# A two-layer hybrid decoder trunk on one core: the order of five engines written out, w1 in two halves, compressed keys in full columns

## The chip, the cores and the metric

The kernel runs on one core of one Trainium2 chip. The metric is the device time of one execution in microseconds (us), taken as the median over several runs. One execution was also recorded by the hardware profiler; every row below is from that record, with times counted from the start of its span.

The engines are called PE (TensorE: matmuls, with their weight loads shown as PEld), DVE (VectorE), ACT (ScalarE), POOL (GpSimd) and SP (SyncE, which here only starts DMAs).

## The reference

Two layers act on x (256 tokens x 1024). Each layer normalises x, projects it once (`z = h @ w_in`) and splits z among three groups of heads, whose gated outputs go through one output projection:

```python
h = rms_norm(x, norm_g); z = h @ w_in
o_a = fox_attention(fq, fk, fv, ff + fox_b) * silu(f_gate)        # 4 heads x 64, forget-gate bias
o_b = conformer_conv(glu_in, ...) * silu(c_gate)                  # GLU, 31-tap conv, LayerNorm, swish, pointwise
o_c = nsa_attention(nq, kc, vc, ks, vs, kw, vw, ...) * silu(n_gate)   # 8 query heads, 2 KV groups, 3 branches
x = x + concat(o_a, o_b, o_c) @ w_out                             # after both layers: a last rms_norm
```

The third group mixes, with sigmoid gates, three attentions: over 15 compressed blocks of keys and values, over selected blocks (with 256 tokens all four are selected) and over a window that here covers everything. The compression takes each 32-token block through a two-layer perceptron: `gelu(blk @ w1) @ w2`, with w1 of 2048 x 256 and w2 of 256 x 64, once for keys and once for values. Everything is float32.

## The kernel before, in words

**Precision by halves.** The large weights are split on the chip into a high part in the fp32r format (a cast on ACT, 128x1024) and a low part (a subtraction on DVE). A product is three matmuls: high x high, high x low, low x high. So every 512 KB block of weights passes one cast on ACT and one subtraction on DVE before PE uses it. `s(i)` is one such block of 128 columns of w_in: 24 matmuls of 256 columns into a PSUM bank that two consecutive `s` share. `mprod` does the same for blocks A and B, `project` for w_out.

**Buffers.** Raw weight blocks come in through SP into `RAW` = 6 buffers, in the order of `queue`; a block's buffer is given back when its low half is formed (`used(1)`), and then the next DMA may go. The blocks of w1 are used raw by PE in `compress(0)` (keys) and `compress(1)` (values), four blocks each, and given back as `compress` consumes them. `HILO` = 8 buffers hold the split halves. PSUM has two banks for `s` and the projections (tag z), three for scores (s), two for transposes (pt), one for attention outputs (o).

**A layer.** After A and B come the `s` blocks: convolution inputs (2 to 5), fox queries and keys (12 to 15), window and selection keys (6, 7), queries (8 to 11), compression inputs (0, 1), and the gates (16 to 23), with the work of the three head groups between them. The third group's attention runs in eight steps n: four heads for the first 128 tokens (t = 0), then four for the second. A step has scores on PE, a mask with maximum on DVE and an exponential on ACT (`exps`), a normalisation on DVE (`norms`), transposes on PE, a copy on ACT, and PV on PE, where `pv(n-1)` and `pv(n)` come together at every odd n. For t = 1 PE alternates these with `project`.

**What sets the order.** In the old kernel PE, SP and POOL follow the order in which the code is written. DVE and ACT do so in layer 0's opening only (the block up to `mprod(0, "B", NB)`); elsewhere a planner, which has its own estimates of durations, picks the order of these two. The forming of weight halves is asked for by `need`, which forms up to `AHEAD` blocks beyond the one wanted, and `behind` holds such an instruction behind marks set by `mark`. At the start PE runs `WARM` idle matmuls (`turn`): five, then eight transposes that spread the first norm gain, then three.

**Around the change.** PE's order there is `s(10)`, `compress(0)`, `fox_pv`, `compress(1)`, `s(11)`, `hidden`, then the first scores and the convolution. `compressed_kv` multiplies w2 with the perceptron's hidden values: for the keys, four matmuls that each fill 64 of PE's 128 columns (two groups, two halves of 256).

Of the kernel before, what the change touches and what calls it, by code (L numbers as in the profile page):

```python
# [9 lines left out]
F32 = mybir.dt.float32  # L10
# [9 lines left out]
AHEAD = 4  # L20
WARM = 5, 3
LAST = 416
LAG = 1
# [38 lines left out]
W2 = {"w2k": (0, 128), "w2v": (128, 128), "pw": (256, 512)}  # L62
W2_N = 768
# [63 lines left out]
def trunk(ctx, tc, a, out, dbg=None):  # L127
    nc = tc.nc
# [8 lines left out]
    ctx.enter_context(tc.manual_schedule(engines={E.SP, E.PE, E.Pool}))  # L137
# [33 lines left out]
    S_ORDER = (2, 3, 4, 5, 12, 13, 14, 15, 6, 7, 8, 9, 0, 1, 10, 11, "w1", 16, 17, 18, 19, 20, 21, 22, 23)  # L171
    queue = []
    parts = []
    for l in range(L):
# [5 lines left out]
        for i in S_ORDER:  # L180
            if i == "w1":
                for m in range(2):
                    for q in range(4):
                        queue.append((("w1", m, q, l), a["w1"][l, m, q], 1024))
# [11 lines left out]
    marks = [{}]  # L196

    def mark():

        at = {}  # L200
        for i in reversed(nc.cur_bb.bb.instructions):
            if i.engine in (E.DVE, E.Activation) and i.engine not in at and i.name not in formed:
                at[i.engine] = i
            if len(at) == 2:
                break
        marks.append(at)

    formed = set()

    def behind(engine, made):  # L210
        at = marks[-LAG].get(engine) if len(marks) >= LAG else None
        with tc.issue_after(at) if at is not None else nullcontext():
            made()
        formed.add(nc.cur_bb.bb.instructions[-1].name)

# [17 lines left out]
    def split_hi():  # L233

        key, n = parts.pop(0)
# [4 lines left out]
        behind(E.Activation, lambda: sc.copy(hi, w))  # L240
        split[key] = hi, lo

        def low():
            behind(E.DVE, lambda: ve.tensor_tensor(lo, w, hi.bitcast(F32), op=ALU.subtract))  # L244
            used(1)
        return low

    def split_next():
        if not parts or parts[0][0] not in raws:
            return False  # L250
        split_hi()()
        return True

    def need(key, ahead=AHEAD):

        while key not in split:
            assert split_next(), key
        n = sum(1 for k in split)
        while n < ahead + 1 and split_next():
            n += 1  # L260
        return split[key]
# [137 lines left out]
    for l in range(L):  # L399
# [17 lines left out]

        def mprod(t, which, n, steps="xt", p=None):
# [18 lines left out]
            if which == "A":  # L437
                sc.copy(vsw[:, t, :], p[:, :256])
                sc.activation(gl[:, t, :], p[:, 256:280], AF.Tanh, scale=0.5)
            else:  # L440
                sc.copy(fv[:, t, :], p[:, :256])
                ve.tensor_tensor(ff[:, t, :], p[:, 256:260], S("fb"), op=ALU.add)


        bank = {}

        def s(i, ahead=AHEAD):

            mark()
            hi, lo = need(("S", i, l), ahead)  # L450
# [11 lines left out]
        def s2(i):  # L462
            return bank.pop(i // 2).rearrange("p (i t) -> p i t", i=2)
# [27 lines left out]
        def gates(i):  # L491
            p = s2(16 + 2 * i)
            u = cp.tile([128, 2, 256], F32, name=nm(f"tg{i}"), tag="tg", bufs=1)
            sc.activation(u, p, AF.Tanh, scale=0.5)
            ve.scalar_tensor_tensor(sgt[0][:, 2 * i:2 * i + 2], u, 1.0, p, op0=ALU.add, op1=ALU.mult)
# [6 lines left out]
        def mix_split(c0, n, cols=slice(0, 256)):  # L502
            m = sgt[0][:, c0:c0 + n, cols]
            h = mixh[:, c0:c0 + n, cols]
            sc.copy(h, m)
            ve.tensor_tensor(mixl[:, c0:c0 + n, cols], m, h.bitcast(F32), op=ALU.subtract)
# [9 lines left out]

        def glu(i):

            p = s2(2 + 2 * i)
            th = cp.tile([128, 512], F32, name=nm(f"th{i}"), tag="tg", bufs=1)[:, 0:256]  # L520
            sc.activation(th, p[:, 1], AF.Tanh, scale=0.5)
            ve.scalar_tensor_tensor(ypad[:, i, 30:286], th, 1.0, p[:, 0], op0=ALU.add, op1=ALU.mult)
# [8 lines left out]
        def taps(i):  # L531
            if i == 0:
                sgt[0] = cp.tile([128, 2, 32, 32], F32, name=nm("cw"), tag="sg", bufs=1)
            cw = sgt[0][:, i]
            behind(E.DVE, lambda: ve.tensor_tensor(
                cw, C("sh").unsqueeze(1).broadcast_to([128, 32, 32]),
                S("cw")[:, i * 32:(i + 1) * 32].unsqueeze(2).broadcast_to([128, 32, 32]), op=ALU.mult))
            pconv[i] = pconv[i], cw.rearrange("p (g q) c -> p g q c", g=4)

        def conv():  # L540
            p = pscore(nm("pcn"))
            for i in range(2):
                yr, w = pconv[i]
                for q in range(8):
                    for g in range(4):
                        te.matmul(p[g * 32:(g + 1) * 32, i * 256:(i + 1) * 256], w[:, g, q], yr[:, g, 4 * q:4 * q + 256],  # L546
                                  start=q == 0, stop=q == 7)
            sgt[0] = cp.tile([128, 8, 256], F32, name=nm("sg"), tag="sg", bufs=1)
            for i in range(2):
                sc.activation(yc[:, i], p[:, i * 256:(i + 1) * 256], AF.Identity, bias=S("cb")[:, i:i + 1])  # L550
# [4 lines left out]
        def ln_stats():  # L555
            pt = ln["p"] = ppt(nm("lnp"))
            st = cp.tile([128, 2, 6], F32, name=nm("st"), tag="st", bufs=1)
            mv = ln["mv"] = cp.tile([128, 2, 2], F32, name=nm("mv"), tag="mv", bufs=1)
            rv = ln["rv"] = cp.tile([128, 2], F32, name=nm("rv"), tag="rv", bufs=1)
            for t in range(2):  # L560
                for c in range(2):
                    o = t * 256 + c * 128
                    te.transpose(pt[:, o:o + 128], yc[:, c, t * 128:(t + 1) * 128], C("id"))
            for t in range(2):
# [3 lines left out]
            gp.tensor_tensor(rv, rv, mhalf[:, :2], op=ALU.pow)  # L568
            yn = ln["yn"] = cp.tile([128, 2, 256], F32, name=nm("yn"), tag="rr", bufs=2)
# [4 lines left out]
        def ln_swish():  # L574
            yn = ln["yn"]
            pn = ppt(nm("lnq"))
# [4 lines left out]
            yl = cp.tile([128, 2, 256], F32, name=nm("yl"), tag="rr", bufs=2)  # L581
# [5 lines left out]
            ve.scalar_tensor_tensor(yt, yt, 1.0, yl, op0=ALU.add, op1=ALU.mult)  # L587

        def pointwise():
# [7 lines left out]
            return pcv.rearrange("p (i t) -> p i t", i=2)  # L597
# [15 lines left out]
        def forget():  # L613
            ffv = ff.rearrange("p t h -> p (t h)")
            lsr = cp.tile([128, 512], F32R, name=nm("lsr"), tag="ru", bufs=2)
            lsh, lsl = (lsr[:, c:c + 256].rearrange("p (t h i) -> p t h i", t=2, h=4) for c in (0, 256))
            fx["ls"] = lsh, lsl
            ve.scalar_tensor_tensor(fa, ffv, -1.0, ffv, op0=ALU.mult, op1=ALU.max)
            sc.activation(fe, fa, AF.Exp, scale=-1.0)
# [631 lines left out]
```

## Time and profile before

| | us |
|---|---|
| median of 3 runs | 316.83 (316.72 to 316.84) |
| the profiled execution | 316.37 |
| its span | 314.6 |
| PE busy | 303.7 |
| DVE busy | 234.9 |
| ACT busy | 186.9 |
| POOL busy | 22.6 |

The span runs from the first to the last recorded instruction; the time of the execution has some 1.8 us more around it. Matmuls overlap their neighbours, so the sum of single durations exceeds the busy time. Busy shares are averages over stages that have different limits, which is why the tables by stretch below matter more than the sums.

### The profile page before, as it was taken

How to read it: one execution, taken by the hardware profiler on the slowest of the kernel's cores; microseconds unless marked ns; L12 is line 12 of the kernel's file. 1: busy time of each engine (PE TensorE's matmuls, PEld its weight loads, DVE VectorE, ACT ScalarE, POOL GpSimd, SP SyncE). 2: the span in 40 equal slices, each digit the busy share in tenths (PEclk: the TensorE clock that was granted, in tenths of full speed). 3: DMA queues.
4: the chain of work that ended last, by engine and by line, in shares of the span. 5: the costliest groups of instructions: out<-in, count | busy, mean ns of one | idle time of the engine just before them, and what ended most of it. 6: DMA issues, size and time to landing. Idle time of an engine off the chain costs nothing.

```text
span 314.6 us, 6713 instructions
## 1 busy us (share of the span) xinstructions
PE 303.7 (97%) x2596; PEld 273.8 (87%) x2596; DVE 234.9 (75%) x626; ACT 186.9 (59%) x408; POOL 22.6 (7%) x49
## 2 busy tenths in 40 slices
PE   7999999999999999999999999999999999999991
PEld 5799999995789999888899999999578999988891
DVE  3957689981999998965574778998199989896532
ACT  4757668731595957861545766783259595786110
POOL 2000043000002000000000003400000200000000
PEclk9999999999999999999999999999999999999998
DMA  7797889707927445130461878880792744000101
GB/s 285 256 382 272 277 246 236 290 2 271 409 69 258 133 135 155 46 94 2 166 200 70 292 233 258 219 307 2 285 403 59 260 135 133 0 2 0 63 8 69
DMA packets 16545, 54.93 MB, mean 175 GB/s; under 512 B 2048, under 2 KB 2560, under 8 KB 16512
## 3 DMA queue, kind: packets, MB, share of 16 engines
q1 hardware_dynamic: 15264, 51.29, 46.9%
q0 software_dynamic: 960, 2.92, 4.1%
q8 instruction: 20, 0.33, 0.4%
q10 hardware_dynamic: 288, 0.28, 0.3%
q14 instruction: 13, 0.11, 0.1%
HBM read 52.85 MB, written 1.64 MB: 173 GB/s over the span
## 4 chain that ended last, share of the span: by engine, by line
PE 88%; issue 4%; DMA 4%; DVE 1%; ACT 1%; POOLq 0%; POOL 0%; DVEq 0%
PE ps L457 15%; PE ps L458 14%; PE ps L459 14%; PE pcn L546 4%; PE pA L430 4%; PE pt L915 4%; PE pB L430 4%; PE pw L982 4%; PE pw L979 4%; PE pw L978 4%; PE on L928 3%; DMA ww<-in_w 3%; PE sw L859 2%; PE sw L860 2%; DMA cf<-in_cf 1%
## 5 line engine op out<-in xcount | busy, mean ns | idle before, releaser
L457 PE MATMUL ps<-hTh,wS_1h 128*128 128x256 f32 x192 | 54.3, 283 | 0.0
L457 PE MATMUL ps<-hTh,wS_0h 128*128 128x256 f32 x192 | 54.3, 283 | 0.0
L459 PE MATMUL ps<-hTh,wS_1l 128*128 128x256 f32 x192 | 53.9, 281 | 0.0
L458 PE MATMUL ps<-hTl,wS_0h 128*128 128x256 f32 x192 | 53.9, 281 | 0.0
L459 PE MATMUL ps<-hTh,wS_0l 128*128 128x256 f32 x192 | 53.9, 281 | 0.0
L458 PE MATMUL ps<-hTl,wS_1h 128*128 128x256 f32 x192 | 53.9, 281 | 0.0
L887 ACT ACTIVATE P<-P,mx 128x128 f32<-128x128 f32 (+1 forms) x64 | 28.5, 447 | 15.1 <-DVE mx L482 15.0
L457 PEld LDWEIGHTS ps<-hTh,wS_1h 128*128 128x128 f32 x192 | 36.2, 188 | 0.6 <-issue 0.4
L457 PEld LDWEIGHTS ps<-hTh,wS_0h 128*128 128x128 f32 x192 | 36.2, 188 | 0.6 <-issue 0.4
L458 PEld LDWEIGHTS ps<-hTl,wS_1h 128*128 128x128 f32 x192 | 36.2, 188 | 0.2
L458 PEld LDWEIGHTS ps<-hTl,wS_0h 128*128 128x128 f32 x192 | 36.2, 188 | 0.2
L459 PEld LDWEIGHTS ps<-hTh,wS_1l 128*128 128x128 f32 x192 | 36.2, 188 | 0.0
L459 PEld LDWEIGHTS ps<-hTh,wS_0l 128*128 128x128 f32 x192 | 36.2, 188 | 0.0
L244 DVE TENSOR_TENSOR wS_0l<-wS,wS_0h 128x1024 fp32r<-128x1024 f32 x24 | 28.6, 1221 | 8.4 <-ACT wS_0h L240 8.4
L244 DVE TENSOR_TENSOR wS_1l<-wS,wS_1h 128x1024 fp32r<-128x1024 f32 x24 | 28.5, 1221 | 8.1 <-ACT wS_1h L240 8.1
L240 ACT CAST wS_1h<-wS 128x1024 fp32r<-128x1024 f32 x24 | 24.1, 1051 | 1.8 <-DMA wS<-in_wS 1.8
L240 ACT CAST wS_0h<-wS 128x1024 fp32r<-128x1024 f32 x24 | 24.1, 1049 | 0.5 <-DMA wS<-in_wS 0.4
L482 DVE CUSTOM_DVE_ANT_0 P<-sw,cf 128x128 f32<-128x128 f32 (+1 forms) x64 | 19.5, 355 | 2.4 <-PE sw L860 2.4
L917 ACT COPY PT<-pt 128x512 f32<-128x512 f32 x24 | 13.6, 586 | 9.6 <-PE pt L915 9.6
L985 DVE TENSOR_TENSOR x<-pw,x 128x512 f32<-128x512 f32 (+1 forms) x9 | 5.7, 631 | 16.8 <-PE pw L982 16.8
L485 DVE TENSOR_SCALAR P<-P,co 128x128 f32<-128x128 f32 (+1 forms) x64 | 16.4, 316 | 0.1
L546 PE MATMUL pcn<-yr,cw 128*32 128x256 f32 x256 | 14.2, 380 | 0.0
(239 smaller groups left out, 679.3 us busy)
## 6 DMA issues: line engine op xcount, KB each, us to landing
wS<-in_wS SPq DMA_DIRECT2D x48, 512.0 KB, 5.7
ww<-in_w SPq DMA_DIRECT2D x16, 512.0 KB, 5.3
wO<-in_wo SPq DMA_DIRECT2D x16, 512.0 KB, 4.0
yr<-ybuf POOLq DMA_DIRECT2D x16, 142.0 KB, 5.0
wA<-in_wA SPq DMA_DIRECT2D x4, 420.0 KB, 4.2
wB<-in_wB SPq DMA_DIRECT2D x4, 390.0 KB, 5.0
x<-in_x SPq DMA_DIRECT2D x2, 512.0 KB, 4.1
w<-in_w SPq DMA_DIRECT2D x2, 384.0 KB, 4.7
```

What stands on the lines that cost most here:

```text
L240: behind(E.Activation, lambda: sc.copy(hi, w))
L244: behind(E.DVE, lambda: ve.tensor_tensor(lo, w, hi.bitcast(F32), op=ALU.subtract))
L430: te.matmul(p[:, :n], a_[:, k, tok], b_, start=first, stop=s_ == "t" and k == 7)
L457: te.matmul(o, hi[:, k], hTh[:, k], start=k == 0, stop=False)
L458: te.matmul(o, hi[:, k], hTl[:, k], start=False, stop=False)
L459: te.matmul(o, lo[:, k], hTh[:, k], start=False, stop=k == 7)
L482: ve.tensor_tensor_reduce(o, x, m, -1.0, 3.0e38, ALU.add, ALU.min, mx)
L485: ve.tensor_scalar(x, x, r, None, op0=ALU.mult)
L546: te.matmul(p[g * 32:(g + 1) * 32, i * 256:(i + 1) * 256], w[:, g, q], yr[:, g, 4 * q:4 * q + 256], start=q == 0, stop=q == 7)
L887: sc.activation(P[:, g, b], P[:, g, b], AF.Exp, bias=mx[:, c:c + 1], scale=-1.0, accum_out=su[:, c:c + 1])
L915: te.transpose(pt[:, o + b * 128:o + (b + 1) * 128], Pg[:, b * 128:(b + 1) * 128], C("id"))
L917: sc.copy(PT, pt)
```

## The change

Five things change.

The first and largest: the order of DVE and ACT is written out for the whole kernel too, and every helper that did work on several engines is cut into pieces that can be placed one by one (`exps` into `mask` on DVE and `expo` on ACT, `norms` into `coeff` and `norms(n, g)`, `trans` into transposes and `ptcopy`, `gates` into `gate_tanh` and `gate_mul`, `query` into `query_rope` and `query(i, g)`, and so on). `need`, `mark` and `behind` go; each half of a weight block is formed where `form_hi` or `form_lo` stands.

```diff
-    ctx.enter_context(tc.manual_schedule(engines={E.SP, E.PE, E.Pool}))
+    ctx.enter_context(tc.manual_schedule(engines={E.SP, E.PE, E.Pool, E.DVE, E.Activation}))
-WARM = 5, 3
+WARM = 8, 1
-    S_ORDER = (2, 3, 4, 5, 12, 13, 14, 15, 6, 7, 8, 9, 0, 1, 10, 11, "w1", 16, 17, 18, 19, 20, 21, 22, 23)
+    S_ORDER = (2, 3, 4, 5, 12, 13, 14, 15, 6, 7, 0, 1, 8, 9, 10, "w1a", 11, "w1b", 16, 17, 18, 19, 20, 21, 22, 23)
...
+    def form_hi():
+        key, n = parts.pop(0)
...
+        sc.copy(hi, w)
+        lows.append((lo, w, hi))
+    def form_lo():
+        if lows:
+            lo, w, hi = lows.pop(0)
+            ve.tensor_tensor(lo, w, hi.bitcast(F32), op=ALU.subtract)
+            used(1)
```

The second: the eight blocks of w1 are queued in two halves with S11 between them, and PE's order follows. S0 and S1 come before S8 and S9. This is the new order around it:

```diff
+        s(8)
+        fox_copy(0, 0)
+        blocks(0)
+        fox_copy(0, 1)
+        form_lo()
+        blocks(1)
+        fox_trans(1, 0)
+        fox_trans(1, 1)
+        form_hi()
+        s(9)
+        fox_copy(1, 0)
+        fox_copy(1, 1)
+        form_lo()
+        s(10)
+        query_rope(0)
+        keys_hi()
+        fox_pv()
+        query(0, 0)
+        query(0, 1)
+        compress(0)
+        keys_lo(0)
+        keys_lo(1)
+        s(11)
+        part(0)
+        taps(0)
+        taps(1)
+        compress(1)
+        query_rope(1)
+        part(1)
+        hidden()
+        query(1, 0)
+        scores(0)
+        load_w2()
+        scores(1)
+        form_hi()
+        conv(0)
+        mask(0, 0)
+        expo(0, 0)
+        branch_gates()
+        mask(0, 1)
+        query(1, 1)
+        expo(0, 1)
+        form_lo()
```

Here `taps` (the convolution's weights, on DVE), `branch_gates` (DVE) and the load of w2 have later places than before. The written order of the steps up to the exponentials of step 3, and of the last two steps, is:

```diff
+        s(19)
+        norms(2, 1)
+        compressed_v()
+        form_lo()
+        ln_back()
+        pv(0)
+        swish_in()
+        mask(3, 0)
+        mask(3, 1)
+        pv(1)
+        trans(2, 0)
+        trans(2, 1)
+        scores(4, (0,))
+        s(20)
+        swish()
+        ptcopy(2)
+        expo(3, 0)
+        expo(3, 1)
+        form_hi()
+        coeff(3)
+        norms(3, 0)
...
+        cmp_norm(1)
+        trans(6, 0)
+        form_lo()
+        trans(6, 1)
+        proj0(1, (0, 1))
+        ptcopy(6, 0)
+        ptcopy(6, 1)
+        coeff(7)
+        norms(7, 0)
+        form_hi()
+        proj0(1, (2, 3))
+        norms(7, 1)
+        form_lo()
+        cmp_trans(1)
+        cmp_copy(1)
+        trans(7, 0)
+        residual(0, 0, 512, pj[0])
+        trans(7, 1)
+        proj0(1, (4, 5))
+        ptcopy(7, 0)
+        ptcopy(7, 1)
+        load_g(a["norm_g"][1] if l == 0 else a["final_g"], nm("gn"))
```

The third: the keys' w2 is stored twice side by side (w2k of 256 columns in place of 128), so that two matmuls with all 128 columns do the work of four with 64; two small copies on ACT pick each group's part.

```diff
-            for g in range(2):
-                for m in range(2):
-                    te.matmul(pk[g * 64:(g + 1) * 64, 0:16], w2k[:, m], gk[:, m, g * 16:(g + 1) * 16],
-                              start=m == 0, stop=m == 1)
+            for m in range(2):
+                te.matmul(pk[:, 0:32], w2k[:, m], gk[:, m], start=m == 0, stop=m == 1)
...
+            kcp = cp.tile([128, 16], F32, name=nm("kcp"), tag="kcp", bufs=1)
+            for g, (r, r2) in enumerate(halves):
+                sc.copy(kcp[r], pk[r, g * 16:(g + 1) * 16])
+            kc = rope(kcp, C("cc"), C("sc"), (16,), "kc")
```

The fourth: the idle matmuls at the start are eight and one in place of five and three. The fifth: `pv(0)` and `pv(1)`, and so on in pairs, stay side by side on PE but with DVE's and ACT's pieces written between them; the last projection's two halves of 256 columns (`proj2`) run all high products of eight k before the low ones.

## Rows read from the trace of the kernel before

**Rows 1.** The page: engines with busy us, share and instructions; PE in 40 slices.

```profile
PE 303.7 (97%) x2596; PEld 273.8 (87%) x2596; DVE 234.9 (75%) x626; ACT 186.9 (59%) x408; POOL 22.6 (7%) x49
...
PE   7999999999999999999999999999999999999991
```

**Rows 2.** Waits: who waited for what, us in total, times, longest us.

```profile
PE ph L791 <- DMA ww<-in_w: 1.3, 2, 0.6
PE g0p L288 <- DMA cf<-in_cf: 1.3, 1, 1.3
```

**Rows 3.** PE in order of time, the compression: start us, us, instruction, [idle before].

```profile
71.23 1.93 PE L791 MATMUL ph<-ww,xp 128*32 128x256 f32 x32
...
74.55 1.59 PE L791 MATMUL ph<-ww,xp 128*32 128x256 f32 x24
76.78 0.64 PE L791 MATMUL ph<-ww,xp 128*32 128x256 f32 x8 [0.65 <-DMA ww<-in_w]
...
80.29 0.97 PE L808 MATMUL hidT<-cf,part 128*128 128x32 f32 x8
```

**Rows 4.** Windows: stretch, length, busy by engine; two `s`, then the two compressions.

```profile
40.98:43.82 2.84, 2.84 (x26) 2.84 (x25) 2.84 (x4) 1.90 (x5) 1.18 (x3) 1.00 1.07 229
77.35:80.29 2.94, 2.94 (x28) 2.94 (x25) 1.16 (x1) 2.39 (x3) 0.00 (x0) 1.00 1.03 414
71.23:73.09 1.86, 1.86 (x33) 0.93 (x32) 0.69 (x2) 0.00 (x0) 0.00 (x0) 1.00 0.29 31
74.55:77.35 2.80, 2.15 (x34) 0.73 (x33) 0.00 (x0) 0.00 (x0) 0.00 (x0) 1.00 1.03 420
```

**Rows 5.** SP's DMA issues in order of time.

```profile
47.71 10.12 SPq L225 DMA_DIRECT2D ww<-in_w  x6
...
71.93 0.80 SPq L225 DMA_DIRECT2D ww<-in_w  x2
```

**Rows 6.** ACT and DVE in order of time, around and after the compression.

```profile
77.49 0.37 ACT L796 COPY part<-ph 128x256 f32<-128x256 f32 x1 [3.88 <-PE ph L791]
79.13 1.23 DVE L244 TENSOR_TENSOR wS_0l<-wS,wS_0h 128x1024 fp32r<-128x1024 f32 x1 [7.20 <-ACT wS_0h L240]
```

**Rows 7.** The chain that ended last, in order of time: start us, us, what.

```profile
93.77 0.35 PE pkv L830 x8
94.12 0.59 PE pkv L833 x4
155.78 0.87 PE hp L354 x8
```

**Rows 8.** Windows: the dense stretch; columns as in rows 4.

```profile
80.50:138.70 58.20, 58.20 (x546) 51.52 (x546) 54.97 (x192) 42.62 (x111) 1.64 (x1) 1.00 0.48 160
```

**Rows 9.** The head: a window, then instructions in order of time.

```profile
7.74:12.70 4.96, 4.56 (x29) 3.25 (x27) 4.39 (x9) 3.01 (x5) 0.55 (x1) 1.00 0.84 306
6.22 1.41 DVE L338 SCALAR_TENSOR_TENSOR h<-x,rs,g0p 128x512 f32<-128x512 f32 x2 [0.67 <-POOL rs L332]
6.32 1.62 PE L282 MATMUL turn<-idle 128*128 128x512 f32 x3
6.84 0.89 ACT L240 CAST wA_0h<-wA 128x840 fp32r<-128x840 f32 x1 [0.39 <-DMA wA<-in_wA]
8.40 1.07 ACT L356 CAST hTh<-hp 128x512 fp32r<-128x512 f32 x2 [0.67 <-PE hp L354]
9.02 0.69 DVE L360 TENSOR_TENSOR hTl<-hp,hTh 128x512 fp32r<-128x512 f32 x1 [0.47 <-ACT hTh L356]
```

**Rows 10.** DVE and PE in order of time: operations that the change moves.

```profile
18.71 0.23 DVE L611 TENSOR_SCALAR gate<-gate,cf 128x8 f32<-128x8 f32 x1
...
120.41 3.49 DVE L244 TENSOR_TENSOR wO_0l<-wO,wO_0h 128x1024 fp32r<-128x1024 f32 x3
140.41 1.17 PE L915 MATMUL pt<-cf,P 128*128 128x128 f32 x8
```

**Rows 11.** DMA issues of the page: KB each, median us from issue to landing.

```profile
gn<-in_norm_g SPq DMA_DIRECT2D x1, 512.0 KB, 7.4
```

More of the change, by code (lines that the diff above doesn't have):

```diff
@@ L61 @@
 SM_N = _o
[L62 to L63 removed]
+W2 = {"w2k": (0, 256), "w2v": (256, 128), "pw": (384, 512)}
+W2_N = 896
 CF = {}
@@ L195, in trunk @@
     raws, split, held = {}, {}, [0]
[L196 to L214, printed above, removed]
     def pump():
@@ L231, in used @@
         pump()
-    def split_hi():
+    lows = []
+    def form_hi():
+        if not parts:
+            return
         key, n = parts.pop(0)
@@ L1051, in trunk @@
[L1051 to L1068 removed]
+        bias_rows()
+        form_hi()
+        s(15)
+        bias_heads()
+        form_lo()
+        form_hi()
+        s(6)
+        fox_k()
+        form_lo()
@@ new lines, in trunk @@
+        mask(1, 0)
+        scores(2)
+        expo(1, 0)
+        mask(1, 1)
+        s(16)
+        form_lo()
+        expo(1, 1)
+        ptcopy(0)
+        coeff(1)
+        norms(1, 0)
+        norms(1, 1)
+        form_hi()
+        ln_trans()
+        form_lo()
+        compressed_kv()
+        s(17)
+        ln_stats()
+        form_hi()
+        mask(2, 0)
+        mask(2, 1)
+        expo(2, 0)
+        expo(2, 1)
+        form_lo()
+        trans(1, 0)
+        trans(1, 1)
+        scores(3)
@@ new lines, in trunk @@
+        expo(3, 0)
+        expo(3, 1)
+        form_hi()
+        coeff(3)
+        norms(3, 0)
+        cmp_scores(0)
+        gate_tanh(1)
+        norms(3, 1)
+        form_lo()
+        scores(4, (1,))
+        form_hi()
+        s(21)
+        cmp_soft(0)
+        gate_mul(1)
+        form_lo()
+        pointwise()
+        mask(4, 0)
+        gate_tanh(2)
+        gate_mul(2)
+        expo(4, 0)
+        trans(3, 0)
+        cmp_norm(0)
+        trans(3, 1)
+        mask(4, 1)
+        form_hi()
@@ new lines, in trunk @@
+        gate_tanh(3)
+        form_lo()
+        pv(3)
+        expo(5, 1)
+        pv_cmp(0)
+        gate_mul(3)
+        trans(4, 0)
+        coeff(5)
+        form_hi()
+        trans(4, 1)
+        norms(5, 0)
+        scores(6, (0,))
+        ptcopy(4, 0)
+        norms(5, 1)
+        proj0(0, (0, 1))
+        mixed(4, 4, on[0], 0.5, TA)
+        ptcopy(4, 1)
+        mix_hi(4, 4, TA)
+        mask(6, 0)
+        mix_lo(4, 4, TA)
+        form_hi()
+        scores(6, (1,))
+        proj0(0, (2, 3))
@@ new lines, in trunk @@
+        form_lo()
+        expo(6, 0)
+        mask(6, 1)
+        trans(5, 0)
+        expo(6, 1)
+        trans(5, 1)
+        form_lo()
+        scores(7, (0,))
+        ptcopy(5, 0)
+        proj0(0, (4, 5))
+        ptcopy(5, 1)
+        coeff(6)
+        norms(6, 0)
+        norms(6, 1)
+        form_hi()
+        scores(7, (1,))
+        cmp_soft(1)
+        proj0(0, (6, 7))
+        form_lo()
+        form_hi()
+        pv(4)
+        mask(7, 0)
+        expo(7, 0)
+        pv(5)
+        mask(7, 1)
```

724 lines of the change are left out of this document (395 added, 329 removed).

## The prediction

> **What bounds the kernel now.** I read the page's first two parts first: PE is busy 303.7 of 314.6 us, nine tenths or more in 38 of 40 slices, and DVE 234.9 us, unevenly spread [rows 1]. A kernel like this gets shorter only by what leaves PE's queue or by PE's own waits. So the second view is what PE and its weight loads waited for: two entries of over a microsecond, the w1 load and cf at the head [rows 2]. PE in order of time shows where: `compress(0)` and `compress(1)` are the same 32 matmuls, and the second breaks off after 24 of them until a DMA lands [rows 3]. Cut to those stretches, the table of windows gives the price: 1.86 us for the undisturbed run, 2.80 for the disturbed one, so 0.94 us a layer, 1.88 in both (the second layer's rows repeat the first's) [rows 4]. The remaining PE idleness is at the head (start to 12.7 us) and behind the last matmul (307.8 to the end), and the change leaves the tail's chain as it is. Everything else in PE's queue touches: a step of `s` follows the one before. So the gain to be had is near 3 us, and the question is whether five hand-written orders give some of it back.
>
> The sum is made against the profiled execution, 316.37 us (span 314.6 and 1.8 around it). The median of the runs is 316.83, 0.46 more, added at the end. With each term stand its ends, the least and the most that it may cost.
>
> **w1 in two halves.** Now six of the eight w1 blocks are issued from 47.7 us on, as raw buffers come free, and the last two only at 71.93, when `compress(0)` has consumed its first block [rows 5]. The last block is in PE at 76.78, 5.55 us after `compress(0)` began (71.23), and the queue moved 420 GB/s meanwhile, which is 1.25 us for a 512 KB block [rows 3, 4]. After the change S11's matmuls stand between the two compressions. The written order forms the low halves of S10 and S11 ahead of `s(10)`, so again two w1 blocks wait for `compress(0)` and no more. Their need moves: `compress(1)` begins 1.86 + 2.94 (an `s` behind narrow matmuls, 77.35 to 80.29 [rows 3]) = 4.80 us after `compress(0)` and needs its last quarter at 4.80 + 3/4 of 1.76 = 6.1 us. Against 5.55 the block is there with 0.57 us to spare. The term: -1.88 us. Its other end: if buffers are handed out in fixed turns, a third block waits, the last lands 1.25 later at 6.8, and 0.7 us of wait stays per layer (term -0.5).
>
> **What this order costs behind it.** `hidden` used to come a whole `s(11)` after `compress(1)`; now it comes at once and reads the copy `part`. That copy starts 77.49 and takes 0.37 [rows 6], so it ends 0.51 us after PE could have gone on at 77.35; `hidden` is eight records in 0.81 us, of which the first half reads the older half of `part` and covers 0.40. I take 0.25 us per layer with the first weight load exposed; ends 0 and 0.6. PE also changes once more between narrow and full column groups: an `s` behind narrow matmuls takes 2.94 against 2.84 behind another [rows 3, 4], so 0.1 per layer; ends 0 and 0.2. Together +0.7.
>
> **Compressed keys in full columns.** Four narrow matmuls (eight records, 0.35 us, 0.044 each) become two full ones (four records). The full ones beside them take 0.117 to 0.15 each [rows 7], so 0.45 to 0.59 against 0.35: 0.1 to 0.24 dearer; on the other side the change of column groups on the way in and out goes, about 0.1 each by the `s` pair above. I take 0; ends -0.25 and +0.25 per layer. The two additional copies of 64x16 on ACT cost less than `part`'s 0.37 each (128x256 [rows 6]). ACT is busy 42.6 of 58.2 us there [rows 8], and the compressed scores come two `s` later; uncovered they would cost up to 0.7 per layer.
>
> The Trainium skill, "TensorEngine Tiling (Array Packing)", section "When to Use Tiling", speaks against this edit: a result of at most 64 columns should be column-tiled for twice the throughput. By it the full form would cost as much again as the narrow one, +0.35 us per layer; the trace's neighbour says 0.1 to 0.24 before the saved switches.
>
> **Head.** The idle turns go from 5 + 3 to 8 + 1. Five turns end with PE waiting 1.27 us for cf; three more at 0.43 each just fill that. After the eight transposes three turns run 6.32 to 7.74 while the first half of h is scaled at 6.92 (6.22 plus half of 1.41): the transposes wait for the turns [rows 9]. With one turn PE is free at 6.9. The high copy of hT on ACT could then start when the cast before it ends, 6.84 + 0.89 = 7.73, not 8.40: up to 0.67. DVE is the tighter one: the low half, at 9.02, finds DVE idle for 0.47 only, since the mean square that ends 8.55, so it and the scale of the second token block behind it move by 9.02 - 8.60 = 0.42, and so do the next transposes (11.37) and everything after. Term -0.42; ends -0.67 and +1.5 (rival C).
>
> **Five written orders.** PE's list is otherwise the old one: s0 and s1 trade places with s8 and s9, `fox_pv` goes ahead of `compress(0)`, and PV already ran in pairs (pv(0) and pv(1) side by side). None of these changes a count, so I cost them at nothing; what hides them is that each operand is ready early. In the front of the layer the two `taps` go out of DVE's way, into its 7.20 us hole before 79.13 [rows 6], and the first fox transposes find their norms about 2 us early by the list.
>
> The dense stretch is 80.5 to 138.7, where DVE works 54.97 of 58.20 us [rows 8]. Now the written order must do there: the same, plus S16's low half (1.23, at 79.13 now [rows 6]) and the branch gates (0.81 for four [rows 10]), less O7's low half and the residual (1.15 and 0.60; three low halves in 3.49 give the first [rows 10]), so 55.3 us. It may start when s(11) ends (80.29 now), after the change a compression earlier; from there to the transposes of step 7, which now start at 140.41 [rows 10], PE has 60.1 + 1.9 + 0.2 = 62.2 us. 6.9 us may be lost to waits in order, against 3.2 now. Going down the written list with these durations I find about 6: 1.5 before the first scores, 1.7 for the swish that waits for `ln_back` behind s(19), 1.5 for the exponentials of step 3 behind the swish on ACT, the rest in pieces. What waits behind those on DVE are low halves and norms due only 1 to 3 us later. So `norms(7)` comes in 0.9 us ahead of its transposes: no PE wait, a small margin. Term 0; ends 0 and +2.5 per layer.
>
> **DMAs moved.** `load_w2` (448 KB for 384) goes from ahead of `compress(0)` to behind `compress(1)`, some 80 us in; at the norm gain's 7.4 us from issue to landing, which was queued in the same place [rows 11], it is there by 88 and needed at 93.8 [rows 7]. The norm gain moves to step 7, behind O7's buffers, about 141.5 + 7.4 = 149; its scaling feeds transposes at 155.8 [rows 7], so nothing; without that cover DVE's queue would stand up to 2 us with the residual behind it.
>
> **Sum.** -1.88 + 0.70 + 0 - 0.42 + 0 + 0 = -1.60; 316.37 - 1.60 = 314.77, and + 0.46 = 315.2 us. Its own range, from the small ends: 314.3 to 316.2.
>
> **Rivals.** A, the slower side: the written DVE order loses more in waits than the planner's, and step 7's transposes wait. Until 0.9 us of delay it is free; beyond that each us costs 2 (two layers). For it: 94% busy DVE, a list that can't take what is ready. Against: the earlier start. With 2.2 us more lost: 315.2 + 2 x 1.3 = 317.8; it makes the kernel slower from about 2.1 us. B: the w1 wait stays because a third block waits, -0.5 in place of -1.88: 316.6. For it: the last block's margin is only 0.57. Against: two slots came free before `compress(0)` in the old order too. C: with one turn PE idles before the first transposes, and the clock's rise comes later. The turns at 6.32 run 0.47 apart where 512 columns later need 0.23, the pace of 1.2 GHz against 2.4; PE's busy time from 7.74 to 12.70 is 4.56 us [rows 9], of which I let a third be paid twice: +1.5 and the 0.42 lost, 317.1. Against: eight turns fill the idle 1.27 us ahead of it. D, the good side: `hidden` and the switches cost nothing and the head gives 0.67, 315.2 - 0.95 = 314.2.
>
> **Chances.** Forecast 0.54, A 0.19, B 0.12, C 0.05, D 0.10. A difference of 0.2% (0.63 us) is what a measurement here can tell: faster is below 316.2, slower above 317.5. Faster: forecast less its edge, and D, 0.61. Within: B, C and that edge, 0.20. Slower: A, 0.19. Range 313.9 to 318.0: D's end to a little beyond A.
>
> **What would show it.** Right: `compress(1)` a run of 1.9 us with no DMA wait; the first transposes near 7.0 and s(2) 0.4 earlier; a gap under 0.4 ahead of `hidden`'s second half; no DVE wait before the transposes of step 7. Wrong: PE idle ahead of any `trans`, a wait for ww in either layer, or a PE wait on ACT in the first fox scores, which I cost at nothing.

## The result, and the profile after

The changed kernel took 315.05 us (median; 313.70 to 319.48) where the kernel before took 317.25 in the same call: ratio 0.992, 95% interval 0.9901 to 0.994. Measured again beside the first experiments it took 314.07 us (313.46 to 315.88) against 317.65, ratio 0.9891 (0.9863 to 0.9919). By the two ratios it is faster by 2.5 and 3.5 us; the intervals reach from 0.6 to 1.4%. The forecast was 315.2 us; its gain over the kernel before was 1.6. Three of its first twenty executions were longer (318.6 to 319.5 us, at a lower mean clock) and are left out of the ratio; the first record is of one of them, so the rows below are from the second record, of 315.88 us, span 314.1, where nothing else is said.

In the rows, `ph` are the compression's matmuls, `ww` its w1 blocks, `fs`, `fP` and `fpt` the fox scores, probabilities and transposes, and `hidT` the matmuls of `hidden`. The page has the same picture as before [rows 1]. PE is busy nearly everywhere, and its busy time is 0.5 us less:

```profile
PE 303.2 (97%) x2589; PEld 274.2 (87%) x2589; DVE 240.3 (77%) x626; ACT 186.9 (59%) x412; POOL 20.8 (7%) x49
...
PE   7999999999999999999999999999999999999991
```

What PE's queue lost and won is seen only in its stretches. These are the windows of the key compression, s(11) and the value compression in layer 0, then both compressions in layer 1 (start to end, length, busy by engine, clock, DMA share, GB/s); they answer to [rows 4]:

```profile
72.54:74.40 1.86, 1.86 (x38) 0.98 (x34) 1.76 (x4) 1.25 (x3) 0.00 (x0) 1.00 0.00 0
74.40:77.45 3.05, 3.05 (x31) 2.83 (x24) 2.74 (x3) 0.37 (x1) 0.00 (x0) 1.00 0.94 334
77.45:79.31 1.86, 1.86 (x35) 1.02 (x33) 1.52 (x4) 0.00 (x0) 0.00 (x0) 1.00 1.01 401
...
220.87:222.73 1.86, 1.86 (x38) 0.99 (x34) 1.76 (x4) 1.29 (x3) 0.00 (x0) 1.00 0.00 0
225.74:228.58 2.84, 2.21 (x35) 0.82 (x33) 2.47 (x5) 0.00 (x0) 0.00 (x0) 1.00 1.03 417
```

In layer 0 the value compression is a clean 1.86 us, 0.94 less than before, as forecast. In layer 1 of this execution it is 2.84 again. The instructions in order of time say why, and they show a second wait that the record of the kernel before does not have, in the first fox scores (start, length, instruction, [idle before, and who ended it]):

```profile
52.01 0.22 PE L691 MATMUL fs<-fk,fq 128*128 128x128 f32 x1
52.91 0.33 PE L692 MATMUL fs<-fklz,fq 128*128 128x128 f32 x1 [0.68 <-POOL fklz L669]
...
221.09 1.93 PE L803 MATMUL ph<-ww,xp 128*32 128x256 f32 x32
225.96 1.64 PE L803 MATMUL ph<-ww,xp 128*32 128x256 f32 x24
228.24 0.64 PE L803 MATMUL ph<-ww,xp 128*32 128x256 f32 x8 [0.63 <-DMA ww<-in_w]
```

The last w1 block was late in layer 1: PE had it 7.15 us after `compress(0)` began (221.09 to 228.24), where the prediction took 5.55 and a margin of 0.57. And POOL's zeroing of the fox keys' low parts (`fklz`) was late, by 0.68 us in layer 0 and 0.21 in layer 1.

The first record (319.48 us) has the same w1 wait in a worse form, two blocks late in layer 1 of the changed kernel; behind it the granted clock is 0.50 of the full 2.4 GHz, the lower level of 1.2, after PE had worked only 1.8 of the 3 us from 225 to 228 (the last row is a window, columns as above):

```profile
227.59 0.64 PE L803 MATMUL ph<-ww,xp 128*32 128x256 f32 x8 [1.17 <-DMA ww<-in_w]
228.85 0.83 PE L803 MATMUL ph<-ww,xp 128*32 128x256 f32 x8 [0.62 <-DMA ww<-in_w]
...
231.00:234.00 3.00, 3.00 (x19) 2.50 (x22) 1.82 (x12) 1.76 (x6) 0.00 (x0) 0.50 0.99 391
```

From the start of `compress(0)` to the first transposes of step 0 layer 1 took 21.2 us, where layer 0 of the same record has 15.9. It is one record; how often this comes is not shown.

For the late zeroing, POOL's queue and SP's:

```profile
50.11 2.19 POOL L506 DMA_DIRECT2D yr<-ybuf  x4 [9.77 <-DMA ybuf<-ypad]
52.34 1.09 POOL L669 MEMSET fklz<- 64x512 f32 x2
```

```profile
38.39 14.01 SPq L203 DMA_DIRECT2D ww<-in_w  x4
```

Before, the same store of the convolution's input came back after 4.42 us and the zeroing ran from 48.80:

```profile
46.58 2.18 POOL L527 DMA_DIRECT2D yr<-ybuf  x4 [4.42 <-DMA ybuf<-ypad]
48.80 1.09 POOL L673 MEMSET fklz<- 64x512 f32 x2
```

The first w1 block is issued at 38.4 where it was 47.7 [rows 5]. I took these early w1 loads for what slows the store, but two runs speak against it. With the w1 edit undone (below) the first w1 block goes at 47.55 again, and the store still takes 7.97 us, in layer 1 9.69. And with the head edit alone, in the planner's order (below), it takes 7.79 and 7.83:

```profile
47.56 2.19 POOL L527 DMA_DIRECT2D yr<-ybuf  x4 [7.79 <-DMA ybuf<-ypad]
```

```profile
47.55 10.11 SPq L225 DMA_DIRECT2D ww<-in_w  x6
```

So neither the early w1 loads nor the written orders are needed for a slow store, and its cause is open. From the first fox scores to the next pair it costs PE 0.87 us in layer 0 and 0.43 in layer 1 of this execution (5.81 and 5.37 us, where the run with the w1 edit undone has 4.94). Without these and the 0.98 of the late w1 block the recorded execution would stand at about 313.6 us (an estimate from these rows), with the lowest of its call, 313.46.

Now the gain that the forecast did not have. The second pair of fox transposes, before and after (PE in order of time):

```profile
64.56 1.07 PE L719 MATMUL fpt<-cf,fP 128*128 128x128 f32 x6
65.38 0.36 PE L457 MATMUL ps<-hTh,wS_0h 128*128 128x256 f32 x1
```

```profile
64.87 0.82 PE L723 MATMUL fpt<-cf,fP 128*128 128x128 f32 x6
65.44 0.36 PE L431 MATMUL ps<-hTh,wS_0h 128*128 128x256 f32 x1
```

From the first transpose to the next `s` it is 0.82 us before and 0.57 after, for the same six instructions, and no row shows an idle time. The first pair went the same way (windows from its first transpose to the next `s`, before and after):

```profile
60.78:61.57 0.79, 0.79 (x9) 0.57 (x7) 0.76 (x4) 0.77 (x2) 0.00 (x0) 1.00 0.76 303
```

```profile
61.13:61.71 0.58, 0.58 (x8) 0.58 (x7) 0.54 (x4) 0.00 (x0) 0.00 (x0) 1.00 0.00 0
```

The norm on DVE explains it; here that of the second pair, first the kernel before, then the one after:

```profile
64.13 1.00 DVE L485 TENSOR_SCALAR fP<-fP,fsu 128x128 f32<-128x128 f32 x4
```

```profile
61.24 1.01 DVE L459 TENSOR_SCALAR fP<-fP,fsu 128x128 f32<-128x128 f32 x4
```

Before, the transposes started at 64.56 while the norm still ran, until 65.13. The norm's quarters end at 64.41, 64.67, 64.87 and 65.13, and the six weight loads of the transposes start at 64.53, then 64.73 and 64.78, then 64.98, then 65.19 and 65.24, each group some 0.1 us behind its quarter: small waits, too short to be listed. After, the norm ends at 62.25, 2.6 us ahead of the transposes, and the loads are an even 0.11 apart. The two pairs give 0.45 us a layer, and the rows of layer 1 repeat it (0.80 and 0.82 before, 0.58 and 0.57 after): 0.9 in both.

At the head, the first transposes start 0.66 us earlier (7.08, before 7.74 [rows 9]), after a wait of 1.01 for h; ACT's copy of hT starts at 7.83 (before 8.40), and the second block's transposes at 10.87 (before 11.37):

```profile
7.08 1.31 PE L324 MATMUL hp<-cf,h 128*128 128x128 f32 x8 [1.01 <-DVE h L308]
7.83 1.19 ACT L326 CAST hTh<-hp 128x512 fp32r<-128x512 f32 x2
...
10.87 1.38 PE L324 MATMUL hp<-cf,h 128*128 128x128 f32 x8
```

In the dense stretch the written order of DVE holds, and not only by the missing idle rows: from the transposes of step 4 to those of step 7 PE takes 15.02 us in layer 0, before 15.04. The norm of step 7 begins 1.04 us ahead of its transposes, which do not wait:

```profile
138.65 1.14 DVE L459 TENSOR_SCALAR P<-P,co 128x256 f32<-128x256 f32 x4
```

```profile
139.69 1.18 PE L942 MATMUL pt<-cf,P 128*128 128x128 f32 x8
```

### The profile page after: what moved, and what is told of

The parts are those of the page before. It is cut to its first block, busy times and chain, and to the rows that moved or that the text cites. A ratio compares the mean times of both kernels' runs of the same rounds, so it can differ in the third digit from the quotient of the medians.

```text
span 317.7 us, 6708 instructions
## 1 busy us (share of the span) xinstructions
PE 305.5 (96%) x2589; PEld 275.7 (87%) x2589; DVE 240.4 (76%) x626; ACT 186.6 (59%) x412; POOL 20.7 (7%) x49
## 4 chain that ended last, share of the span: by engine, by line
PE 88%; issue 4%; DMA 4%; ACT 1%; DVE 1%; POOLq 0%; SPq 0%; POOL 0%; DVEq 0%
PE ps L431 14%; PE ps L433 14%; PE ps L432 14%; PE pcn L524 5%; PE pA L402 4%; PE pt L942 4%; PE pB L402 4%; PE pw L1018 4%; PE pw L1017 4%; PE pw L1021 4%; PE on L962 3%; DMA ww<-in_w 2%; PE sw L882 2%; DMA wA<-in_wA 2%; PE sw L883 2%
## 5 line engine op out<-in xcount | busy, mean ns | idle before, releaser
L524 PE MATMUL pcn<-yr,cw 128*32 128x256 f32 x256 | 15.5, 404 | 0.0
L524 PEld LDWEIGHTS pcn<-yr,cw 128*32 128x32 f32 x256 | 8.3, 117 | 6.6 <-issue 1.6
```

The source lines that it names most:

```text
L524: te.matmul(pconv["p"][g * 32:(g + 1) * 32, i * 256:(i + 1) * 256], w[:, g, q], yr[:, g, 4 * q:4 * q + 256], start=q == 0, stop=q == 7)
```

## The experiments

Each was timed in five rounds beside the kernel before.

**The changed kernel again.**

> The changed kernel itself, run beside the next three on one chip so that each can be set against it. By all theories it stays 1.5 to 2.7 us below the kernel before (its ratio was 0.990 to 0.994). In its record I look for what the written account of the gain needs: both runs of the value compression at 1.9 us without a wait for a w1 block, both groups of fox transposes at 0.57 us (0.79 and 0.82 before), and s(2) no earlier than before, since the cast of wA's first part may again wait for its DMA.

314.07 us, ratio 0.9891 (0.9863 to 0.9919). Its record is the one above. The value compression was clean in one layer only, which I had not expected, and the head came out earlier, not equal. The executions range over 2.4 us; the recorded one, with both waits, is the longest of the six.

**The w1 edit alone, in the kernel before.**

```diff
-    ... 8, 9, 0, 1, 10, 11, "w1", 16, ...
+    ... 8, 9, 0, 1, 10, "w1a", 11, "w1b", 16, ...
-        compress(0)
         fox_pv()
-        compress(1)
+        compress(0)
         s(11, 1)
+        compress(1)
```

> The kernel before with the w1 edit alone: S11 queued between the two halves of w1, PE's order fox PV, key compression, s(11), value compression; DVE and ACT stay with the planner, the idle turns are five and three, the keys narrow. Theory 1 (the w1 wait is most of the gain): the 1.9 us of both layers go, and 0.2 to 0.5 come back at the copy ahead of hidden and at the change of column groups: 1.4 to 1.7 us faster than the kernel before. Theory 2 (the gain lies in the written order of DVE and ACT): the wait only moves to another place, within 0.5 us of the kernel before. Theory 3 (the last block is late again where the planner forms the halves at other times): 0.3 to 0.9 us faster, with a wait for a w1 block left in the value compression.

330.57 us, ratio 1.0343 (1.029 to 1.0396): about 11 us slower by the ratio, 13 in the recorded execution (330.83 us), which no theory had. ACT in order of time, then PE, show the two places in layer 0:

```profile
51.99 1.05 ACT L240 CAST wS_0h<-wS 128x1024 fp32r<-128x1024 f32 x1
60.70 1.05 ACT L240 CAST wS_0h<-wS 128x1024 fp32r<-128x1024 f32 x1 [7.66 <-DMA wS<-in_wS]
61.65 0.40 ACT L706 ACTIVATE fP<-fP,fmx 128x128 f32<-128x128 f32 x1
...
86.26 1.04 ACT L240 CAST wS_0h<-wS 128x1024 fp32r<-128x1024 f32 x1 [5.08 <-DMA wS<-in_wS]
87.21 0.37 ACT L796 COPY part<-ph 128x256 f32<-128x256 f32 x1
```

```profile
65.62 1.41 PE L719 MATMUL fpt<-cf,fP 128*128 128x128 f32 x6 [4.40 <-DVE fP L485]
...
87.63 0.63 PE L808 MATMUL hidT<-cf,part 128*128 128x32 f32 x4 [1.43 <-ACT part L796]
```

With four w1 blocks queued ahead of it, S11 is there only at 60.7. In the planner's order its cast stands on ACT ahead of the fox exponentials, where it also stood in the kernel before, when the data was there. Now ACT stands still for 7.66 us, the exponentials come late, DVE's norm comes late, and PE waits 4.40. The same happens at S16's cast, ahead of the copy of part.

The waits are not all of it. In this record PE waits some 10 us longer than in the record before, and it is also busy 4.1 us longer (307.8 for 303.7), with a lower granted clock behind the long wait. The same stretch in this run and in the kernel before:

```profile
65.60:71.00 5.40, 5.38 (x31) 5.13 (x32) 4.99 (x14) 3.09 (x10) 0.00 (x0) 0.68 0.25 99
```

```profile
65.60:71.00 5.40, 5.40 (x48) 5.40 (x47) 3.85 (x9) 1.80 (x4) 0.00 (x0) 1.00 0.00 0
```

At 0.68, between the levels of 1.2 and 2.4 GHz, PE gets 31 records done where it gets 48 at 1.00.

**The head alone, in the kernel before** (`WARM = 8, 1`).

> The kernel before with eight idle turns and one in place of five and three. My prediction gave this edit -0.42 us. Theory 1 (after the record of the changed kernel): between -0.4 and +0.3 us, because the first transposes come 0.5 us earlier but the cast of wA's first part on ACT, which stands ahead of the copy of hT, waits for its DMA, so s(2) does not come earlier. Theory 2 (the head carries a real part of the gain, since the clock rises sooner): 0.8 us faster or more, with s(2) starting before 22.7 us.

317.29 us, ratio 0.9985 (0.9968 to 1.0002): about 0.5 us faster, against the 0.42 of the forecast, with an interval that just takes in no difference. Its record (317.21 us) holds something else, a wait in layer 1 that the record of the kernel before lacks, though from here on both have the same order. ACT, DVE and PE in order of time:

```profile
228.17 1.05 ACT L240 CAST wS_1h<-wS 128x1024 fp32r<-128x1024 f32 x1 [1.57 <-DMA wS<-in_wS]
```

```profile
229.25 1.23 DVE L244 TENSOR_TENSOR wS_1l<-wS,wS_1h 128x1024 fp32r<-128x1024 f32 x1 [8.51 <-ACT wS_1h L240]
```

```profile
240.00 0.39 PE L859 MATMUL sw<-kh,qs 128*128 128x256 f32 x1 [0.74 <-DVE qs L761]
```

In the record before, this cast waited 0.19 us only and began at 227.20; here S16 is 1 us late, DVE's queue with the second query behind it shifts by as much, and PE waits 0.74 at the third scores, and a little at the transposes ahead of them. The kernel before runs between 316.1 and 318.7 us in these calls, and the record that I worked from, of 316.37 us, was near the lower end. That this wait is what its longer executions have is likely, but shown for one execution only.

**The w1 edit undone, in the changed kernel.**

```diff
-    ... 8, 9, 10, "w1a", 11, "w1b", 16, ...
+    ... 8, 9, 10, 11, "w1a", "w1b", 16, ...
```

with PE's order as before, `compress(0)`, `fox_pv`, `compress(1)`, `s(11)`.

> The changed kernel with the w1 edit taken back: w1 in one piece behind S11, PE's order key compression, fox PV, value compression, s(11); the written orders, the eight and one turns and the full-column keys stay. Theory 1: the waits for w1 blocks come back, 0.9 us a layer, less the 0.2 to 0.3 a layer that the uncovered copy ahead of hidden cost: 1.2 to 1.9 us slower than the changed kernel in the same call, so only 0.6 to 1.3 us faster than the kernel before. Theory 2 (the written orders are the gain): within 0.5 us of the changed kernel.

315.19 us, ratio 0.9915 (0.9891 to 0.9939): 1.1 us slower than the changed kernel in the same call, a little below what theory 1 gave and beyond theory 2. The waits are back, 0.8 us in layer 0 (2.66 from the first matmul of the value compression to s(11)), and what the w1 edit costs behind it is gone:

```profile
76.53 0.64 PE L803 MATMUL ph<-ww,xp 128*32 128x256 f32 x8 [0.58 <-DMA ww<-in_w]
77.10 0.39 PE L431 MATMUL ps<-hTh,wS_0h 128*128 128x256 f32 x1
```

So the edit is worth 1.1 us, where I had 1.88 - 0.70 = 1.18. The two intervals overlap, so the medians alone do not settle it; the records agree: from the second fox transposes to the first transposes of step 0 this run takes 24.25 and 24.31 us in the two layers, and a layer of the changed order with no w1 wait 23.76 (both layers of the run with the early zeros, below). That is 0.5 a layer. Undoing the edit still leaves 2.5 us between this kernel and the one before: the larger part is not w1. Its fox transposes take 0.58 and 0.57 us, so that gain belongs to the written orders.

**The same as the second run, with the casts asked for later.**

```diff
-        s(9) ... s(0) ... s(1) ... s(11, 1)
+        s(9, 3) ... s(0, 2) ... s(1, 1) ... s(11, 0)
```

> The kernel before with the w1 edit alone, as in the second run (13 us slower than before), and one thing more: the casts of S11 and S16 on ACT are asked for later, S11's behind s(1) and S16's behind s(11), so that they no longer stand in ACT's queue ahead of the fox exponentials and of the copy of part. Theory 1 (the edit itself is worth its wait, and it failed because the planner put a cast that waits for its DMA ahead of work that PE needs): the stalls of 4.6 us ahead of the first fox transposes and of 1.4 us in hidden go, and the kernel comes out between 1.7 us faster and 0.5 us slower than before. Theory 2 (w1 loads that start 5 us earlier take the DMA queues from S10 and S11, whatever ACT's order): PE waits for S10 or S11 itself, and the kernel stays 4 us or more slower than before.

329.34 us, ratio 1.039. This decides nothing: the planner put both casts back in the same places of ACT's order, and the waits are nearly the same (6.4 us on ACT, up to 4.2 on PE). A later run asks the question from the other side.

**The zeros early.**

```diff
-            fx["kl"] = [cp.tile([128, 2, 256], F32R, ..., tag="xp", bufs=2) for g in range(2)]
+            kl = cp.tile([128, 2, 2, 2, 256], F32R, ..., tag="sg", bufs=1)
+            fx["kl"] = [kl[:, 0, g] for g in range(2)]
...
         forget_sum()
+        fox_k0()
         glu_tanh(0)
```

> The changed kernel with the low parts of the fox keys in a buffer of their own (the one of the mixed outputs, free at that time), zeroed on POOL ahead of glu(0), where the changed kernel zeroes them behind glu(1), in the buffer that the convolution's store must give back. Theory 1 (w1 loads that start at 38 us in place of 47.7 slow that store from 4.4 to 8 or 10 us, and in some executions the zeroing comes too late for the first fox scores, 0.7 us in the record with 315.88 us, part of the spread between executions): up to 1.3 us less in the executions that had this wait, 0 in the others, so a median 0 to 0.7 us below the changed kernel's, and no wait of PE on POOL left. Theory 2 (the spread has only to do with w1's last block): no difference beyond 0.2 us.

314.31 us (313.81 to 314.48), ratio 0.9902 (0.9881 to 0.9923). The wait on POOL is gone from both layers and the range is 0.7 us wide where it was 2.4, but the median is not lower than the 314.07 of the changed kernel. That the late zeroing costs PE time is borne out, and its weight is that of a few executions. That the early w1 loads make it late is not: without them the store was as slow.

**The value compression later.**

```diff
         s(11)
+        scores(0)
+        scores(1)
...
         compress(1)
...
-        hidden()
-        scores(0)
-        scores(1)
...
         conv(0)
...
+        hidden()
...
         conv(1)
```

This is PE's order alone; DVE's and ACT's masks and exponentials of steps 0 and 1 move with it.

> The changed kernel with the value compression behind the first two scores (1.1 us later) and hidden between the two halves of the convolution; on DVE the masks of step 0 go ahead of the second query's rotation, those of step 1 ahead of a low half. Theory 1 (the last w1 block's margin of 0.6 us is used up in some executions, and the copy of part is uncovered): 0.22 us a layer from hidden, and the w1 waits of 0.98 us and more in layer 1 go: 0.4 to 1.5 us below the changed kernel, with a narrower spread. Theory 2 (a longer wait for masks takes their place, since the convolution's bank is the one of the first scores): PE waits on DVE ahead of the convolution, and the time is the changed kernel's or up to 1 us above.

313.06 us (312.82 to 313.78), ratio 0.9871 (0.9849 to 0.9894): 1.25 us below the run with the early zeros in the same call, and 1.0 below the 314.07 that the changed kernel had in another (0.6 by the ratios). Both compressions of layer 1 are now clean:

```profile
219.27 1.93 PE L803 MATMUL ph<-ww,xp 128*32 128x256 f32 x32
...
225.09 1.93 PE L803 MATMUL ph<-ww,xp 128*32 128x256 f32 x32
```

One half of the expectation failed. `hidden` was to give back 0.22 us a layer once its copy was ready early. The copy was ready at 79.81 (ACT, in order of time) and `hidden` began at 82.6, but it still takes 1.01 us (window, columns as above), where it took 0.81 behind s(11):

```profile
79.44 0.37 ACT L811 COPY part<-ph 128x256 f32<-128x256 f32 x1 [0.38 <-PE ph L803]
```

```profile
82.61:83.62 1.01, 1.01 (x13) 0.86 (x8) 0.88 (x3) 0.20 (x1) 0.00 (x0) 1.00 0.95 369
```

What stands ahead of it here is the convolution, and in the changed kernel the compression: both use PE in column groups of 32. The waits of its weight loads (us in total, times, longest) are the same in both kernels, and the kernel before has no such row:

```profile
PEld hidT L823 <- issue: 0.8, 2, 0.4
```

So the 0.22 us comes with the change from column groups of 32, not with the copy.

Not all of the gain is a w1 wait avoided. The record with the early zeros has no such wait either, and it takes 23.76 us from the second fox transposes to the first transposes of step 0 in each layer, where this one takes 23.58 and 23.57: 0.4 us in both layers come with the new order itself, and what makes them is not shown.

**Both of these together.**

> The last two edits together. If both mechanisms hold and are separate, their gains add: 0.6 to 2 us below the changed kernel, 312.5 to 313.8 us where the kernel before has 316.8 to 317.7, and an execution-to-execution spread under 1 us. If they share one cause (the w1 loads' traffic), the sum is no more than the better of the two.

313.52 us (313.24 to 313.73), ratio 0.9877 (0.9856 to 0.9898). The gains do not add. Against the early zeros alone the later compression gives 0.8 us here, with ranges that do not meet (313.81 to 314.48 there, 313.24 to 313.73 here). The zeros bring a narrower spread to the changed kernel and nothing more; in both records with them the time behind the last matmul is 0.35 us longer (7.40 us, 7.05 in the others), which takes from their gain.

**One cast moved ahead, in the changed kernel.**

```diff
         fox_mask(3)
-        fox_exp(3)
         form_lo()
+        form_hi()
+        fox_exp(3)
         fox_norm(1)
...
         fox_trans(1, 1)
-        form_hi()
         s(9)
```

> The changed kernel with one cast on ACT moved: S11's high half stands ahead of the fox exponentials of head 3 in place of behind the second pair of fox transposes' predecessors (the two copies of the first pair). It puts a cast whose DMA lands at 64.3 us ahead of an exponential that ran at 60.0, as the planner's order did in the second run. (The fifth run was to test this from the planner's side, but the planner put both casts back where they were.) Theory 1 (a w1 load ahead of S11 is safe only if ACT's order keeps S11's cast out of the way; in the planner's order that cast cost the 13 us): the exponential, the norm behind it and on DVE all that is queued behind that norm, S10's low half too, come 5 us later; PE waits 2 us a layer at the second fox transposes and up to 5 us in all by s(10): 4 to 10 us slower than the changed kernel. Theory 2 (the 13 us came from the DMA traffic of the early w1 loads, which is the same here as in the changed kernel): within 0.7 us of the changed kernel.

322.56 us (322.34 to 322.76), ratio 1.0165 (1.0149 to 1.018): 8.5 us slower than the changed kernel, in theory 1's range. The chain in layer 0, from ACT over DVE to PE:

```profile
63.46 1.05 ACT L222 CAST wS_0h<-wS 128x1024 fp32r<-128x1024 f32 x1 [4.32 <-DMA wS<-in_wS]
64.42 0.40 ACT L711 ACTIVATE fP<-fP,fmx 128x128 f32<-128x128 f32 x1
```

```profile
65.43 0.18 DVE L715 RECIPROCAL fsu<-fsu 128x4 f32<-128x4 f32 x1 [5.33 <-ACT fP L711]
```

```profile
66.07 1.07 PE L723 MATMUL fpt<-cf,fP 128*128 128x128 f32 x6 [2.00 <-DVE fP L459]
```

In layer 0 PE waits another 1.3 us ahead of s(10), for DVE; in layer 1 it waits 2.73 at the transposes, and the granted clock is 0.56 in the 3.3 us behind them. One instruction in another place costs 8.5 us in two layers, with the same loads and the same matmuls. That is the mechanism of the second run's loss, shown without the planner; that it makes up all of it there is not shown.

**The better version again, and two small parts undone in it.** First the version with the later value compression once more:

> The version with the later value compression once more, beside the next two, which undo one small part of the change in it; its executions differ by only 1 us, so terms of 0.3 us can be told. All theories: 1.0 to 1.3% below the kernel before, 312.8 to 313.8 us.

313.32 us (313.04 to 313.37), ratio 0.9872 (0.9857 to 0.9887). Then the narrow keys (four matmuls of 64 columns, no copies):

> That version with the compressed keys in two groups of 64 columns again (four matmuls, no copies on ACT). My prediction costed the full columns at 0, ends -0.25 and +0.25 per layer. Theory 1 (the record: 0.81 us for the stretch in either form): within 0.3 us of the version with full columns. Theory 2 (by the Trainium skill, TensorEngine Tiling (Array Packing), When to Use Tiling, a result this small should be column-tiled): 0.7 us faster with the narrow form.

313.07 us (312.80 to 314.13), ratio 0.9872 (0.985 to 0.9894): no difference that can be told. The stretch is 0.81 us in both forms, so the price of the full columns is 0, as in the forecast. The Trainium skill ("TensorEngine Tiling (Array Packing)", "When to Use Tiling") would column-tile a result of this width, as the narrow form does. No gain from that shows in these runs (313.07 us narrow, 313.32 full). Last the idle turns, five and three:

> That version with five and three idle turns again in place of eight and one. My prediction gave the edit -0.42 us, and the kernel before with this edit alone was 0.15% faster (0.5 us; interval from no difference to 1.0). Theory 1: 0.2 to 0.7 us slower than the version with eight and one. Theory 2 (the start of the DMAs sets the head, not the turns): within 0.2 us.

313.88 us (313.71 to 313.99), ratio 0.9889 (0.9872 to 0.9907): 0.56 us slower than eight and one, in theory 1's range.

## Why the prediction was right, point by point

The time came out right (315.05 and 314.07 for 315.2), the gain too small, 1.6 where 2.5 to 3.5 were measured. That the time came so near is in part luck: the kernel before measured 0.4 and 0.8 us above the 316.83 that I started from, and the 0.9 us that I missed at the fox transposes made up for that.

**The w1 wait, -1.88.** Right where the block is in time: 0.94 in layer 0. The queue did what was forecast: two blocks are issued only when `compress(0)` has consumed its first. The margin of 0.57 us was too thin: in layer 1 of both records of the changed kernel the wait came back, in the records with the early zeros or the later compression it did not. Rival B's wait thus comes in some executions and one layer, by another cause than a third block behind the buffers: two blocks waited, and the last was there after 7.15 us, where I had 5.55. Why the DMA takes longer there is not settled.

**What the order costs behind it, +0.70.** The size of the first part was right (0.22 a layer for 0.25), the cause was wrong: not the copy but the column groups, which I had put at 0.1. With s(11) at 3.05 and 3.01 for 2.94 [rows 4] the sum is 0.62 in two layers. The net of the edit is 1.1 us by the medians with it undone, 1.0 by the records.

**The head, -0.42.** Measured 0.5 and 0.56 us, by two edits in opposite directions, of which the second is clear of the noise. Rival C did not come: the granted clock reads 1.00 from 0.9 to 12.7 us, before and after.

**Compressed keys, 0.** Measured 0.

**Five written orders, 0.** This is the term that failed, in both directions. Its upper end of +2.5 was for waits that did not come: no PE wait for DVE stands in the dense stretch, and norms(7) begin 1.04 us ahead as forecast (0.9); rival A is out. But the gain of 0.9 us at the fox transposes was missed, although the prediction says that their norms come 2 us earlier. The step that failed is "Everything else in PE's queue touches": I took a stretch without idle rows for a stretch at full speed. The six transposes at 0.82 us stood in the record before, beside a norm that ended 0.57 us after they began.

The second fault is in the parts' independence. I costed the w1 edit by itself at -1.2, as if it could be made in either order. In the planner's order it costs 11 to 13 us. Its cover is the place of S11's cast on ACT, behind the exponentials; that place was part of the "order" which I costed at nothing, and one moved line takes 8.5 us. I named what hides the move, and what it costs without that cover, for the DMAs and not for this cast.

**DMAs moved, 0.** Right for w2 and the norm gain. Incomplete for the rest: I counted w1's blocks by need and did not ask when the first ones would start (9 us earlier), nor for how long the convolution's store may take. It took 4.4 and 5.0 us in the record that I worked from and up to 9.8 in the others, and the wait that follows from it, 0.7 us in one record, I had at nothing.

The sum of what the runs show, from the kernel before: -1.1 for w1, -0.5 for the head, -0.9 for the fox transposes, 0 for the keys, together -2.5. That is as much as the first measurement (0.8% of 317 us), but the parts were measured in other calls, and in the second measurement the whole was 3.5. The 1 us more there is not accounted for; the wait at the third scores that one record of the old order shows (1.2 us with the transposes ahead of it) would fill it, but no run here tests that.

## What to carry to other kernels

A stretch without idle rows can still be slow: compare the time of the same group of instructions in two places or two layers, and look whether the engine that feeds it ends after the group begins. On an engine that works in order, each cast that waits for a DMA is a lock on all behind it; when a load is put ahead of another in a queue, look up where the delayed block's first user stands and what is behind it there. And a margin of half a microsecond against a DMA is met in some executions and missed in others, so move the user, not the load: here 1.1 us later went with 0.8 us less (between the two runs with early zeros), though half of that stands in records without any w1 wait.

## What the runs showed of the hardware

A store of 144 KB from POOL (the second of a layer) came back after 4.4 and 5.0 us in the record of the kernel before, after 7.8 in the same kernel with the head edit alone, and after 7.4 to 9.8 in the records of the written orders, whether the w1 loads start at 38 us or at 47.6; what holds it up is not settled. The 0.2 us at `hidden` behind groups of 32 columns was there in both places, behind the compression and behind the convolution. A long wait of PE cost more than its length: behind 4.40 us without work the granted clock was 0.68 over the next 5.4 us, where the kernel before has 1.00. And the range was 2.4 us over six executions of the changed kernel and 1.0 over five with the later compression: in the one record that I could take apart, the longest of the six, what looks like noise was waits for DMAs that landed 1 us later.
